# A decoder layer on one core: three value chunks and a gate chunk made as pairs by seven products, and three activation chunks split straight from PSUM

## The chip, the cores and the metric

The kernel runs on one core of a Trainium2 chip. The metric is device time in microseconds (us): the median of three runs of the kernel before was 1387.82 us (1387.64 to 1389.24). The profile shows one further execution of the same program. Its engines are named PE (matmul; PEld is its weight load), DVE (vector), ACT (scalar), POOL (GpSimd, here an issuer of DMAs) and SP (the issuer of the weight loads).

## What is computed

One layer of a decoder over 256 positions of width 2048, in float32. Cut to what matters:

```python
h = rmsnorm(x, g_mix)
proj = h @ w_in                                  # 2048 x 12288: q, k, v of 16 heads, then 3 gates of 2048
q, k, v = ...                                    # 16 heads of 128: groups 0 to 3 of four heads
gates = sigmoid(proj[..., 3 * MIX_WIDTH:])
o_a = stick_breaking_attention(q[:4], k[:4], v[:4])                     # group 0
o_b, o_c = moba_attention(...), dilated_attention(...)                  # groups 1 to 3, softmax with biases
merged = gates[0] * (o_a @ w_branch_a) + gates[1] * (o_b @ w_branch_b) + gates[2] * (o_c @ w_branch_c)
x = x + merged @ w_out
gu = rmsnorm(x, g_ffn) @ w_gu                    # 2048 x 11264
x = x + (silu(gu[..., :5632]) * gu[..., 5632:]) @ w_down
```

## The kernel before

Weights arrive from DRAM in blocks of 256 rows by 512 columns (a tile 128x1024, 512 KB). To keep float32 accuracy each block is split in two parts by `split` (lines 104 to 107): ACT writes a rounded copy `w_hi`, DVE the rest `w_lo`; the activations are kept as such parts too. `product` (line 164) then issues three matmuls of 512 columns, lines 167 to 169: high by high, high by low, low by high.

A chunk of 512 output columns is made in one of two ways.

- `project`, the plain way: 16 row tiles of the weights times 2 halves of the positions, 32 products, 96 matmuls, with 8 blocks split.
- `project_pair` makes two chunks at once. Over half of the rows (the chunks `WC` of the activations) it makes seven products of sums in place of eight of blocks, in the manner of Strassen and Winograd: `form` is one of the seven (12 matmuls), `rest` a plain block of the other half. That is 180 matmuls for two chunks, 22 splits, six additions of weight blocks on DVE (lines 321 and 310), two more by an accumulating DMA that POOL issues (line 360), four copies of PSUM banks by ACT (`snapshot`, line 305) and four additions of 128x512 that combine the results (lines 367, 369, 372, 380). `begin_pair` starts the loads and splits of the next pair ahead of time.

`units` sets the order of the projection: v of group 0, a gate chunk, q and k of groups 0 and 1 (a pair each, "qk"), v1, qk2, v2, qk3, v3, a gate chunk, and then the other gate chunks in pairs. Attention is woven in between: it is written as generators (`attention`, `rows_to_columns`) in the list `slow_stages`; `parts`, which splits a block, advances that list at every second call. Group g's attention is put in the list by `keep_v`, once v of the group is there. From the pair `chunks[4]` on, the list is drained and the attention's PSUM is given to `acc2`.

After the branches and the output projection come the eleven pairs over `w_gu` (loop over c, line 942). Each gives one chunk c of 512 columns of the activation a = silu(g) * u. `to_a` transposes it on PE into PSUM, copies it with ACT into SBUF (line 938) and sends it to the DRAM tensor `a_mem` by POOL's queue (line 939). `take_a` reads a chunk back (line 959, `a_raw<-a_mem`, 512 KB) and splits it into `a_hi` and `a_lo` for the down projection. It is called right behind the loop for the first three chunks (`EARLY`), whose tiles lie in the pool `pe`, and later for the rest. The instructions are not issued in the order in which they are written: a scheduler puts each engine's list in an order of its own when the program is built, and each engine then executes its list in that order. `tc.keep_in_program_order` pins some of them.

Of the kernel before, what the change touches and what calls it, by code (L numbers as in the profile page):

```python
# [9 lines left out]
F32 = mybir.dt.float32  # L10
# [7 lines left out]
P = 128  # L18
D = 2048
S = 256  # L20
NT = S // P
# [33 lines left out]
def hybrid_block(ctx: ExitStack, tc: tile.TileContext, x, g_mix, w_in, q_gain, k_gain, w_branch, w_out,  # L55
# [82 lines left out]
    def finish_stages(queue):  # L138
        while queue:
            advance(queue)  # L140
# [612 lines left out]
    def attention(g, qT, kT, v):  # L753
        biases = []
        if g:
            for hl in (0, 2):
                bias = pa.tile([P, 2, S], F32, name="bias")
                nc.gpsimd.dma_start(bias, bass.AP(tensor=vec.tensor, offset=vec.offset + (4 * g - H_A + hl) * NDIST,
                                                  ap=[[1, P], [NDIST, 2], [1, S]]))
                biases.append(bias)  # L760
        for hl in (0, 2):
            if g:
                yield from softmax_pair(4 * g + hl, hl, qT, kT, v, biases[hl // 2])
            else:
                yield from stick_breaking(hl, qT, kT, v)
            yield
# [9 lines left out]
    heads = {}  # L776

    def keep_v(g, ps):
        finish_stages(slow_stages)
        heads["v", g] = v = pa.tile([P, NT, NB], F32, name="v", bufs=1)  # L780
        for t in range(NT):
            nc.scalar.activation(v[:, t, :], ps[t], AF.Copy, scale=rstd[:, t:t + 1])
        if g:
            slow_stages.append(attention(g, *heads["qk", g], v))

    def keep_qk(g, q0, q1, k0, k1):
        sbs = []
        for t, (src, own) in enumerate(((q0, True), (q1, False), (k0, True), (k1, True))):
            sb = src if own else half_kb()
            nc.scalar.activation(sb, src, AF.Copy, scale=rstd[:, t % NT:t % NT + 1])  # L790
            sbs.append(sb)
        heads["qk", g] = qkT = [pa.tile([P, 4, S], F32, name=f"{n}T") for n in "qk"]
        if g:
            stages.append(rows_to_columns(g, sbs, qkT))
        else:
            slow_stages.append(rows_to_columns(g, sbs, qkT))
            slow_stages.append(attention(g, *qkT, heads["v", g]))

    chunks = [(c, b) for c in range(4) for b in range(3)]
    units = [("v", 0), ("gate", chunks[0]), ("qk", 0), ("qk", 1), ("v", 1), ("qk", 2), ("v", 2), ("qk", 3), ("v", 3)]
    units += [("gate", chunks[1])] + [("gates", chunks[i:i + 2]) for i in range(2, len(chunks), 2)]

    def gate_col(c, b):
        return 3 * NH * HD + b * D + c * NB

    def pair_of(kind, what):
        if kind == "qk":
            return hs, w_in, what * NB, NH * HD + what * NB  # L810
        if kind == "gates":
            return hs, w_in, gate_col(*what[0]), gate_col(*what[1])

    def in_turn():
        turn.reverse()
# [11 lines left out]
    others = in_turn  # L827
    ahead = None
    for (kind, what), after in zip(units, units[1:] + [(None, None)]):
        if kind == "gates" and what[0] == chunks[4]:  # L830
            finish_stages(slow_stages)
            pat.close()
            acc2 = ctx.enter_context(tc.tile_pool(name="acc2", bufs=1, space=PSUM))
            others = beside
            o = Columns(pool(ph1, "o", "left"), "o", NH)
            stages.append(split_o())
        nxt = pair_of(*after)
        if kind in ("qk", "gates"):
            ps, ahead = project_pair(*pair_of(kind, what), ahead, nxt)
            if others is in_turn:  # L840
                turn.reverse()
        else:
            ps = project(h, 0, w_in, 0, KT, V0 + what * NB if kind == "v" else gate_col(*what),
                         *((ps0, 4, there) if (kind, what) == ("v", 0) else ()))
            ahead = begin_pair(*nxt) if nxt else None
        finish_stages(stages)
        if kind == "v":
            keep_v(what, ps)
            if what == 0:
                slow_stages.append(sums_of_h())  # L850
        elif kind == "qk":
            keep_qk(what, *ps)
        elif kind == "gate":
            keep_gate(*what, ps)
        else:
            keep_gate(*what[0], ps[:2])
            keep_gate(*what[1], ps[2:])
# [73 lines left out]

    a_mem = dram.tile([NF // 4, P, 4, S], F32, name="a_mem")

    def to_a(c, srcs):
        for t in range(NT):
            pt = transpose4(srcs[t])
            st = half_kb().rearrange("p (k q) -> p k q", k=4)
            nc.scalar.copy(st, pt)
            nc.gpsimd.dma_start(a_mem[c, :, :, t * P:(t + 1) * P], st)
            yield  # L940
# [7 lines left out]
            nc.vector.scalar_tensor_tensor(sg[t], u, rstd2[:, t:t + 1], sg[t], op0=ALU.mult, op1=ALU.mult)  # L948
        stages.append(to_a(c, sg))

    WD = (4, 6, 8)
    ORDER = [0, 1, 2, 4, 3, 6, 5, 8, 7, 9, 10]
    EARLY = 3
    a = Chunks(None, "a", NF // 4, WD, False)

    def take_a(pl, c):
        a.place(pl, c)
        raw = pr.tile([P, 4, S], F32, name="a_raw", bufs=2)
# [6 lines left out]
        else:  # L965
            split(*a.t[c], raw)

    for c in ORDER[:EARLY]:
        take_a(pe, c)
    h2_stack.close()  # L970
    pd = pool(ctx, "pd", "left")

# [143 lines left out]
```

## Time and profile before

| What | Value |
|---|---|
| median of 3 runs | 1387.82 us |
| the profiled execution | 1387.56 us, its span 1385.8 us |
| PE busy | 1362.3 us (98%), 6404 matmuls |
| DVE busy | 1151.7 us (83%) |
| ACT busy | 880.9 us (64%) |
| POOL busy | 109.4 us (8%) |
| granted PE clock, mean | 0.994 |
| bytes moved by DMA | 331.07 MB |

The projections of `w_in` fill the span up to about 530 us, the branches and the output projection the time to about 700 us, the eleven pairs of `w_gu` the time to about 1160 us, and the down projection the rest. PE is near full everywhere, so what counts is where it is not: the rows on its waits and on the granted clock.

### The profile page before, as it was taken

To read this page: it belongs to the slowest core of one execution; us is meant where nothing else is said; L and a number is where in the kernel's file an instruction comes from. 1 tells how busy PE (TensorE), PEld (TensorE's weight loads), DVE (VectorE), ACT (ScalarE), POOL (GpSimd) and SP (SyncE) were. 2 spreads that over 40 slices of the span, in tenths; PEclk is the share of its full clock that TensorE was granted. 3 is DMA by queue.
4 is the path that set the end of the run, shared out by engine and by line. 5 is a ranking of instruction groups with operands and counts; after the bars stand their busy time and mean duration, and the time that the engine had idled before them with its cause. 6 is when DMAs were issued, how large, how long until landed. Compare 5 with 4: busy or idle time off the path is not lost.

```text
span 1385.8 us, 17910 instructions
## 1 busy us (share of the span) xinstructions
PE 1362.3 (98%) x6404; PEld 1184.9 (85%) x6404; DVE 1151.7 (83%) x1222; ACT 880.9 (64%) x1140; POOL 109.4 (8%) x173
## 2 busy tenths in 40 slices
PE   9999999999999999999999988999999999999998
PEld 7888888888888888888887877888888888788887
DVE  7888797858989987776698877999999998887785
ACT  7678877767776665445565656667666665564553
POOL 1100000000010112101001001010000010100000
PEclk9999999999999999999999999999999999999999
DMA  8875567576687779877887677678787877767553
GB/s 277 288 255 169 202 181 257 147 242 196 244 286 266 263 228 336 276 220 227 294 276 252 224 244 228 214 259 285 247 277 244 274 216 236 258 239 258 195 178 101
DMA packets 93928, 331.07 MB, mean 239 GB/s; under 512 B 11312, under 2 KB 12928, under 8 KB 93840
## 3 DMA queue, kind: packets, MB, share of 16 engines
q1 hardware_dynamic: 76896, 275.29, 57.1%
q0 software_dynamic: 15760, 53.60, 15.0%
q8 instruction: 50, 0.82, 0.2%
q10 hardware_dynamic: 1184, 1.06, 0.2%
q14 instruction: 38, 0.31, 0.1%
HBM read 292.65 MB, written 16.27 MB: 223 GB/s over the span
## 4 chain that ended last, share of the span: by engine, by line
PE 77%; issue 12%; DMA 4%; ACT 3%; DVE 3%; POOL 1%; POOLq 0%; ACTq 0%; DVEq 0%
PE ps L167 9%; PE ps L168 9%; PE ps L169 9%; PE qs L169 9%; PE qs L168 9%; PE qs L167 9%; PE z L167 4%; PE z L169 4%; PE z L168 4%; DMA a_raw<-a_mem 2%; PE v L167 2%; PE v L168 2%; PE v L169 2%; PE tr L189 1%; ACT w_hi L105 1%
## 5 line engine op out<-in xcount | busy, mean ns | idle before, releaser
L105 DVE TENSOR_TENSOR w_lo<-w_raw,w_hi 128x1024 fp32r<-128x1024 f32 x334 | 405.2, 1221 | 84.7 <-ACT w_hi L105 81.9
L105 ACT CAST w_hi<-w_raw 128x1024 fp32r<-128x1024 f32 x334 | 347.4, 1048 | 177.3 <-PE qs L169 80.1
L105 ACT CAST w_hi<-g_raw 128x1024 fp32r<-128x1024 f32 x184 | 191.5, 1048 | 137.0 <-DVE g_raw L310 45.8
L105 DVE TENSOR_TENSOR w_lo<-g_raw,w_hi 128x1024 fp32r<-128x1024 f32 x184 | 221.3, 1222 | 37.3 <-ACT w_hi L105 34.1
L105 ACT CAST w_hi<-u 128x1024 fp32r<-128x1024 f32 x138 | 143.8, 1047 | 82.9 <-PE qs L169 17.8
L105 DVE TENSOR_TENSOR w_lo<-u,w_hi 128x1024 fp32r<-128x1024 f32 x138 | 167.8, 1221 | 27.4 <-ACT w_hi L105 26.6
L168 PE MATMUL ps<-w_lo,h_hi 128*128 128x512 f32 x360 | 136.7, 380 | 0.0
L169 PE MATMUL ps<-w_hi,h_lo 128*128 128x512 f32 x360 | 136.4, 379 | 0.0
L167 PE MATMUL ps<-w_hi,h_hi 128*128 128x512 f32 x360 | 134.0, 383 | 0.0
L168 PE MATMUL qs<-w_lo,h_hi 128*128 128x512 f32 x332 | 126.4, 381 | 0.0
L169 PE MATMUL qs<-w_hi,h_lo 128*128 128x512 f32 x332 | 125.9, 380 | 0.0
L167 PE MATMUL qs<-w_hi,h_hi 128*128 128x512 f32 x332 | 122.5, 381 | 0.0
L169 PEld LDWEIGHTS ps<-w_hi,h_lo 128*128 128x128 f32 x360 | 68.0, 189 | 9.6
L168 PEld LDWEIGHTS ps<-w_lo,h_hi 128*128 128x128 f32 x360 | 68.1, 189 | 9.3
L167 PEld LDWEIGHTS ps<-w_hi,h_hi 128*128 128x128 f32 x360 | 67.8, 189 | 9.2
L321 DVE TENSOR_TENSOR u<-g_raw 128x1024 f32<-128x1024 f32 x40 | 48.8, 1219 | 26.7 <-DMA g_raw<-in_w_in 18.6
L169 PEld LDWEIGHTS qs<-w_hi,h_lo 128*128 128x128 f32 x332 | 62.8, 189 | 9.4 <-issue 0.6
L168 PEld LDWEIGHTS qs<-w_lo,h_hi 128*128 128x128 f32 x332 | 62.8, 189 | 9.0 <-DVE w_lo L105 0.4
L167 PEld LDWEIGHTS qs<-w_hi,h_hi 128*128 128x128 f32 x332 | 62.7, 189 | 8.6
L167 PE MATMUL v<-w_hi,h_hi 128*128 128x512 f32 x120 | 47.7, 397 | 13.3 <-ACT w_hi L105 13.3
L310 DVE TENSOR_TENSOR u<-u,g_raw 128x1024 f32<-128x1024 f32 x40 | 47.2, 1219 | 0.0
L310 DVE TENSOR_TENSOR g_raw<-g_raw 128x1024 f32<-128x1024 f32 x40 | 47.1, 1218 | 0.0
(398 smaller groups left out, 2950.2 us busy)
## 6 DMA issues: line engine op xcount, KB each, us to landing
w_raw<-in_w_in SPq DMA_DIRECT2D x118, 512.0 KB, 4.7
g_raw<-in_w_gu SPq DMA_DIRECT2D x88, 512.0 KB, 6.1
w_raw<-in_w_gu SPq DMA_DIRECT2D x88, 512.0 KB, 6.6
g_raw<-in_w_in SPq DMA_DIRECT2D x72, 512.0 KB, 6.2
w_raw<-in_w_down SPq DMA_DIRECT2D x64, 512.0 KB, 4.3
u<-g_raw POOLq DMA_DIRECT2D x40, 512.0 KB, 5.5
w_raw<-in_w_branch SPq DMA_DIRECT2D x32, 512.0 KB, 4.8
w_raw<-in_w_out SPq DMA_DIRECT2D x32, 512.0 KB, 4.3
```

Source lines behind the costliest of these rows:

```text
L105: for op in nc.scalar.copy(hi, src), nc.vector.tensor_sub(lo, src, hi.bitcast(F32)):
L167: nc.tensor.matmul(ps, ah, wh, start=start, stop=False, **how)
L168: nc.tensor.matmul(ps, ah, wl, start=False, stop=False, **how)
L169: nc.tensor.matmul(ps, al, wh, start=False, stop=stop, **how)
L189: nc.tensor.transpose(pt[:, i, :], src[:, i * P:(i + 1) * P], ident)
L310: tc.keep_in_program_order(nc.vector.tensor_add(d, d, a))
L321: nc.vector.tensor_add(d, a, b)
```

## The change

There are two parts.

1. v of groups 1 and 2 become one pair ("vv"), and v of group 3 with the gate chunk `chunks[1]` another ("vg"). v of group 2 is made ahead of qk2; until it is used it lies in the four heads of `o_raw` that group 3's output takes later. Attention of a group is put in the list by `attend`. The drain of `slow_stages` comes where v1, v2's attention and the pair `chunks[8]` need it; the attention's PSUM is handed over at `chunks[8]` in place of `chunks[4]`.
2. The first three chunks of a that the down projection takes are placed ahead of the loop, and `to_a` splits them from PSUM: no copy to SBUF, no trip to `a_mem` and back.

```diff
     def keep_v(g, ps):
-        finish_stages(slow_stages)
-        heads["v", g] = v = pa.tile([P, NT, NB], F32, name="v", bufs=1)
+        if g == 2:
+            v = o_raw[:, 12:16, :].rearrange("p h q -> p (h q)").rearrange("p (t n) -> p t n", t=NT)
+        else:
+            if g == 1:
+                finish_stages(slow_stages)
+            v = pa.tile([P, NT, NB], F32, name="v", bufs=1)
+        heads["v", g] = v
         for t in range(NT):
             nc.scalar.activation(v[:, t, :], ps[t], AF.Copy, scale=rstd[:, t:t + 1])
-        if g:
-            slow_stages.append(attention(g, *heads["qk", g], v))
+
+    def attend(g):
+        slow_stages.append(attention(g, *heads["qk", g], heads["v", g]))
...
-    units = [("v", 0), ("gate", chunks[0]), ("qk", 0), ("qk", 1), ("v", 1), ("qk", 2), ("v", 2), ("qk", 3), ("v", 3)]
-    units += [("gate", chunks[1])] + [("gates", chunks[i:i + 2]) for i in range(2, len(chunks), 2)]
+    units = [("v", 0), ("gate", chunks[0]), ("qk", 0), ("qk", 1), ("vv", (1, 2)), ("qk", 2), ("qk", 3)]
+    units += [("vg", (3, chunks[1]))] + [("gates", chunks[i:i + 2]) for i in range(2, len(chunks), 2)]
...
-        if kind == "gates" and what[0] == chunks[4]:
+        if kind == "gates" and what[0] == chunks[8]:
             finish_stages(slow_stages)
             pat.close()
...
-        if kind in ("qk", "gates"):
+        if kind in ("qk", "gates", "vv", "vg"):
             ps, ahead = project_pair(*pair_of(kind, what), ahead, nxt)
...
+        elif kind == "vv":
+            keep_v(1, ps[:2])
+            keep_v(2, ps[2:])
+            attend(1)
         elif kind == "qk":
+            if what == 3:
+                finish_stages(slow_stages)
+                attend(2)
             keep_qk(what, *ps)
+        elif kind == "vg":
+            keep_v(3, ps[:2])
+            keep_gate(*what[1], ps[2:])
+            attend(3)
...
+    for c in ORDER[:EARLY]:
+        a.place(pe, c)
+
     def to_a(c, srcs):
         for t in range(NT):
             pt = transpose4(srcs[t])
+            if c in ORDER[:EARLY]:
+                a.put(c, t, pt)
+                yield
+                continue
             st = half_kb().rearrange("p (k q) -> p k q", k=4)
             nc.scalar.copy(st, pt)
             nc.gpsimd.dma_start(a_mem[c, :, :, t * P:(t + 1) * P], st)
             yield
...
-    for c in ORDER[:EARLY]:
-        take_a(pe, c)
     h2_stack.close()
```

The order of the instructions moves at three places. The first is ACT's list in the second pair over `w_gu`. Names: `w_raw` and `g_raw` are weight blocks as loaded, `u` a sum of two, `w_hi` their rounded part, `tr` a PSUM bank with transposes, `sc` a scratch tile, `z` and `ps` PSUM banks; the number behind a name tells one tile from the next. Before:

```order
L938 COPY sc_6723<-tr_6718 128x512
L938 COPY sc_6741<-tr_6736 128x512
L105 CAST w_hi_6794<-u_6660 128x1024
L305 COPY sc_6750<-z_6686 128x512
L105 CAST w_hi_6804<-u_6661 128x1024
L105 CAST w_hi_6820<-w_raw_6818 128x1024
L105 CAST w_hi_6838<-g_raw_6648 128x1024
L105 CAST a_hi0_10162<-a_raw_10164 128x1024
L105 CAST w_hi_6848<-g_raw_6650 128x1024
L105 CAST w_hi_6862<-w_raw_6860 128x1024
```

With the change:

```order
L105 CAST a_hi0_6387<-tr_6797 128x4x128
L105 CAST a_hi0_6387<-tr_6814 128x4x128
L105 CAST w_hi_6871<-u_6739 128x1024
L305 COPY sc_6827<-z_6765 128x512
L105 CAST w_hi_6881<-u_6740 128x1024
L105 CAST w_hi_6897<-w_raw_6895 128x1024
L105 CAST w_hi_6915<-g_raw_6727 128x1024
L105 CAST w_hi_6925<-g_raw_6729 128x1024
L105 CAST w_hi_6939<-w_raw_6937 128x1024
```

The split of the reloaded chunk, which stood between two weight splits, is gone; the rounded part is taken from PSUM where the copy to scratch stood. The same holds for the third and fourth pair.

The second place is DVE's list at the end of the pair qk1, where the plain chunk v1 followed and now the pair vv begins (`p` with `att` is attention of group 0):

```order
 L372 TENSOR_TENSOR sc<-ps,sc 128x512
-L105 TENSOR_TENSOR w_lo<-w_raw,w_hi 128x1024 x4
+L105 TENSOR_TENSOR w_lo<-w_raw,w_hi 128x1024
+L321 TENSOR_TENSOR u<-g_raw 128x1024 x2
+L105 TENSOR_TENSOR w_lo<-w_raw,w_hi 128x1024
+L105 TENSOR_TENSOR w_lo<-g_raw,w_hi 128x1024 x2
 L664 TENSOR_TENSOR p<-p,att 128x768
```

Two additions of weight blocks for the next pair now stand here, among the splits.

The third is POOL's list over the pairs with attention: `bias` is a table for attention that one of two buffers takes, `u<-g_raw` the accumulating DMA of a pair.

```order
 L774 DMA gate_mem<-sc 128x512 x2
-L360 DMA u<-g_raw 128x1024 x4
+L360 DMA u<-g_raw 128x1024 x6
 L758 DMA bias<-vec 128x2x256
 L360 DMA u<-g_raw 128x1024 x2
-L758 DMA bias<-vec 128x2x256 x2
+L758 DMA bias<-vec 128x2x256
+L360 DMA u<-g_raw 128x1024 x2
+L758 DMA bias<-vec 128x2x256
 L360 DMA u<-g_raw 128x1024 x2
```

The pair vv puts two accumulating DMAs ahead of the third `bias`, and two more now stand between the fourth and the fifth.

More of the change, by code (lines that the diff above doesn't have):

```diff
@@ L796, in keep_qk @@
             slow_stages.append(rows_to_columns(g, sbs, qkT))
-            slow_stages.append(attention(g, *qkT, heads["v", g]))
+            attend(g)
     chunks = [(c, b) for c in range(4) for b in range(3)]
-    units = [("v", 0), ("gate", chunks[0]), ("qk", 0), ("qk", 1), ("v", 1), ("qk", 2), ("v", 2), ("qk", 3), ("v", 3)]
-    units += [("gate", chunks[1])] + [("gates", chunks[i:i + 2]) for i in range(2, len(chunks), 2)]
+    units = [("v", 0), ("gate", chunks[0]), ("qk", 0), ("qk", 1), ("vv", (1, 2)), ("qk", 2), ("qk", 3)]
+    units += [("vg", (3, chunks[1]))] + [("gates", chunks[i:i + 2]) for i in range(2, len(chunks), 2)]
     def gate_col(c, b):
@@ L812, in pair_of @@
             return hs, w_in, gate_col(*what[0]), gate_col(*what[1])
+        if kind == "vv":
+            return hs, w_in, V0 + what[0] * NB, V0 + what[1] * NB
+        if kind == "vg":
+            return hs, w_in, V0 + what[0] * NB, gate_col(*what[1])
     def in_turn():
@@ L932, in hybrid_block @@
     a_mem = dram.tile([NF // 4, P, 4, S], F32, name="a_mem")
+    WD = (4, 6, 8)
+    ORDER = [0, 1, 2, 4, 3, 6, 5, 8, 7, 9, 10]
+    EARLY = 3
+    a = Chunks(None, "a", NF // 4, WD, False)
+    for c in ORDER[:EARLY]:
+        a.place(pe, c)
     def to_a(c, srcs):
@@ L949, in hybrid_block @@
         stages.append(to_a(c, sg))
[L951 to L954, printed above, removed]
     def take_a(pl, c):
```

## The prediction

> **What bounds the kernel.** I read the page first, then PE's waits, then the timeline around the longest one, then the windows by stage.
>
> ```profile
> span 1385.8 us, 17910 instructions
> PE 1362.3 (98%) x6404; PEld 1184.9 (85%) x6404; DVE 1151.7 (83%) x1222; ACT 880.9 (64%) x1140; POOL 109.4 (8%) x173
> ```
>
> PE is the bound. Time can come from fewer matmuls, from its idle time (1385.8 less 1362.3, 23.5 us) or from a fuller clock. The list of PE's waits names one row that matters (total, times, longest):
>
> ```profile
> PE v L167 <- ACT w_hi L105: 13.3, 4, 4.2
> ```
>
> Three of the four are alike. Around the first, the timelines of ACT, POOL and PE (start, duration, what; in brackets the idle time ahead of it and who ended it):
>
> ```profile
> 754.40 1.04 ACT L105 CAST w_hi<-g_raw 128x1024 fp32r<-128x1024 f32 x1 [2.69 <-DVE g_raw L310]
> 759.96 1.04 ACT L105 CAST a_hi<-a_raw 128x1024 fp32r<-128x1024 f32 x1 [4.51 <-DMA a_raw<-a_mem]
> 760.91 1.04 ACT L105 CAST w_hi<-g_raw 128x1024 fp32r<-128x1024 f32 x1
> ...
> 747.60 1.62 POOL L939 DMA_DIRECT2D a_mem<-sc  x2 [32.20 <-ACT sc L938]
> 754.42 0.56 POOL L959 DMA_DIRECT2D a_raw<-a_mem  x1 [2.62 <-PE z L169]
> ...
> 758.40 0.38 PE L169 MATMUL z<-w_hi,h_lo 128*128 128x512 f32 x1
> 762.95 0.79 PE L167 MATMUL v<-w_hi,h_hi 128*128 128x512 f32 x1 [4.18 <-ACT w_hi L105]
> 763.54 0.63 PE L167 MATMUL z<-w_hi,h_hi 128*128 128x512 f32 x1
> 763.97 0.63 PE L167 MATMUL ps<-w_hi,h_shi 128*128 128x512 f32 x1
> ```
>
> A chunk of a is written to DRAM at 747.60 and read back at 754.42. ACT stands before the split of the reloaded chunk, with the weight splits queued behind it, until 759.96; PE has used up what was split and waits 4.18 us. Then its matmuls start 0.43 us apart instead of 0.22. The windows by pair, from transpose to transpose (length, then busy time and count of PE, PEld, DVE, ACT and POOL, then PE's granted clock, DMA share, GB/s), show the price: three disturbed pairs, one undisturbed, all with 189 matmuls, and the slow piece behind the first wait.
>
> ```profile
> 746.08:792.86 46.78, 42.60 (x189) 36.59 (x188) 38.13 (x36) 27.51 (x31) 3.83 (x5) 0.93 0.69 225
> 792.86:838.49 45.63, 41.39 (x189) 35.75 (x188) 37.78 (x36) 27.51 (x31) 3.83 (x5) 0.96 0.70 231
> 838.49:885.16 46.67, 42.47 (x189) 36.51 (x188) 37.91 (x36) 27.50 (x31) 3.84 (x5) 0.93 0.68 226
> 885.16:924.89 39.73, 39.73 (x189) 34.82 (x188) 36.61 (x35) 26.68 (x30) 3.29 (x4) 1.00 0.76 252
> ...
> 762.95:768.23 5.28, 5.28 (x12) 4.20 (x13) 4.24 (x5) 3.37 (x4) 0.00 (x0) 0.50 0.51 161
> ```
>
> **Part 1, the activation chunks.** The three disturbed pairs take 46.78 + 45.63 + 46.67 = 139.08 us, against 3 x 39.73 = 119.19. If nothing else holds them, 19.89 us come back: about 12.6 of idle PE (three waits of 4.2) and 7.3 of half clock. ACT's list, shown above, no longer has the split that waited: the chunk's new splits stand where the copies to scratch stood, released by the same transposes. What they cost, by these groups (mean ns behind the busy time):
>
> ```profile
> L938 ACT COPY sc<-tr 128x512 f32<-128x512 f32 x22 | 12.9, 589 | 14.0 <-PE tr L189 13.4
> L105 ACT CAST m_hi<-tr 128x512 fp32r<-128x512 f32 x8 | 4.3, 593 | 0.1
> L105 DVE TENSOR_TENSOR m_lo<-tr,m_hi 128x512 fp32r<-128x512 f32 x8 | 5.1, 682 | 0.0
> L105 DVE TENSOR_TENSOR a_lo<-a_raw,a_hi 128x1024 fp32r<-128x1024 f32 x8 | 9.8, 1223 | 18.1 <-ACT a_hi L105 18.1
> ```
>
> The output projection's input is already split from PSUM in this form, at 593 ns on ACT and 682 ns on DVE. Six ACT copies (589) become six ACT splits (593), and three ACT splits of a reloaded block go: ACT gains. DVE has 2 x 0.68 = 1.36 us in each pair where 1.22 stood. Beside the undisturbed 36.61 that is 37.97 of 39.73 us, 95.6% busy. One pair in the trace is as dense:
>
> ```profile
> 706.40:746.08 39.68, 39.06 (x179) 33.06 (x177) 38.57 (x47) 27.59 (x31) 1.78 (x2) 1.00 0.85 293
> ```
>
> 38.57 us of DVE in 39.68, with 0.62 us of PE idle. So the new splits cost from nothing to 0.62 in each pair; I take 0.5 in all. The DMAs that go (six writes and three reads on POOL's queue) have nothing but the accumulating DMA behind them; they are worth nothing more. The transposes' PSUM bank is held 0.68 us longer; the next transposes are a pair away.
>
> The clock belongs to the saving, so a rule is weighed here. The row has 5.28 us at 0.50 behind the first wait. The Trainium skill (TensorE: Matmul & The Clock Gate, Part 1) says that PE falls to half clock after an idle window of some 3.4 us and regains it after about as long at work. The trace agrees on the halving. By that figure a stall would cost, as an estimate, 4.2 us and half of 3.4, the three 17.7 us in place of 19.9, and the forecast would be 2.2 us higher.
>
> **Part 2, the pairs.** Two plain chunks are 192 matmuls, a pair 180; two pairs save 24. A pair of gate chunks without attention gives the price, 38.85 us for 180 matmuls, 0.2158 each:
>
> ```profile
> 449.20:488.05 38.85, 38.85 (x181) 34.02 (x180) 34.90 (x33) 26.50 (x31) 4.02 (x6) 1.00 0.81 270
> ```
>
> So 24 x 0.2158 = 5.18 us go from PE. SP loads the same 16 blocks for two chunks either way.
>
> The other engines get more. Each new pair adds on DVE six splits, six block additions and four additions of 128x512; on ACT six splits and four bank copies; on POOL two DMA issues.
>
> ```profile
> L105 DVE TENSOR_TENSOR w_lo<-u,w_hi 128x1024 fp32r<-128x1024 f32 x138 | 167.8, 1221 | 27.4 <-ACT w_hi L105 26.6
> L367 DVE TENSOR_TENSOR sc<-sc 128x512 f32<-128x512 f32 x20 | 13.7, 685 | 0.9 <-ACT sc L305 0.9
> L105 ACT CAST w_hi<-u 128x1024 fp32r<-128x1024 f32 x138 | 143.8, 1047 | 82.9 <-PE qs L169 17.8 <-PE ps L169 15.1 <-DVE u L1016 14.0
> L305 ACT COPY sc<-qs 128x512 f32<-128x512 f32 x35 | 20.3, 581 | 3.0 <-PE qs L169 2.8
> 925.57 2.35 DVE L310 TENSOR_TENSOR u<-u,g_raw 128x1024 f32<-128x1024 f32 x2
> ```
>
> Two block operations in a row take 2.35 us, so the second adds 1.13. DVE gets 12 x 1.13 to 1.22 and 4 x 0.685 per pair, 16.3 to 17.4; I take 33.8 us for both. ACT gets 6 x 1.05 + 4 x 0.58 = 8.6, 17.2 for both. The place is the stretch from the end of qk0 to the end of the first gate pair; the second row reaches to the end of the gates, the third is the densest undisturbed stretch of the later stages.
>
> ```profile
> 93.67:371.25 277.58, 276.01 (x1355) 241.53 (x1354) 221.88 (x277) 209.49 (x364) 11.05 (x14) 1.00 0.63 205
> 93.67:526.90 433.23, 430.94 (x2070) 376.43 (x2069) 360.88 (x404) 316.50 (x485) 28.13 (x40) 1.00 0.69 224
> 1000.00:1050.00 50.00, 50.00 (x241) 43.84 (x241) 46.70 (x45) 34.91 (x41) 5.75 (x7) 1.00 0.72 238
> ```
>
> Afterwards the stretch has 277.6 - 5.2 = 272.4 us for PE and 221.9 + 33.8 = 255.7 us for DVE: 93.9%, where 46.70 of 50 us, 93.4%, ran with no PE idle. ACT has 226.7, 83%. DVE is thus just within what it has carried, and some attention can move into the later gate pairs, since the list is now drained at `chunks[8]`. A good part of DVE's idle time before was the plain chunks' own:
>
> ```profile
> 146.39 1.23 DVE L321 TENSOR_TENSOR u<-g_raw 128x1024 f32<-128x1024 f32 x1 [5.92 <-DMA g_raw<-in_w_in]
> 356.22 1.23 DVE L321 TENSOR_TENSOR u<-g_raw 128x1024 f32<-128x1024 f32 x1 [0.62 <-DMA g_raw<-in_w_in]
> ```
>
> At 146 us, in the plain v1, DVE waits 5.92 us for the next pair's blocks; where a pair follows a pair, 0.62. The new waits cost, below, -2.3 us (the PE idle of the long stretch, 433.23 less 430.94, vanishes); above, if DVE could again be used only 221.88/277.58 = 80%, 255.7/0.80 = 319.9 us, 42.3 more than before. The nearest row is the dense one without PE idle, so I take 1.0.
>
> POOL's two more issues per pair hide in an engine that is 8% busy. They stand behind `bias` loads that wait for attention:
>
> ```profile
> 177.00 0.74 POOL L758 DMA_DIRECT2D bias<-vec  x1 [70.22 <-DVE p L689]
> 178.13 0.86 POOL L360 DMA_DIRECT2D u<-g_raw  x1 [0.39 <-DVE w_lo L105]
> ```
>
> The `bias` load waited 70.22 us, and the accumulating DMA behind it went 0.39 us after that by a later DVE instruction. In the new list one `bias` stands before each pair's two again, and in DVE's list the read that frees it precedes the split that frees `u`: no cost. Without that cover `u` comes late and PE waits, at the price of a stall (below).
>
> **The sum**, on the profiled execution of 1387.56 us (0.26 below the median of the runs): 1387.56 - 19.89 + 0.5 - 5.18 + 1.0 = 1363.99. I say 1364.
>
> **Rivals.**
> A. One or two real stalls in the dense stretch. A disturbed pair costs (139.08 - 119.19)/3 = 6.63 us, idle and half clock. For it: DVE near full, attention's tied chain of ACT and DVE, scratch and PSUM shared with a pair at work. Against: two operations of blocked ACT or DVE are covered by five buffers of split weights. Without waits the time is 1362.5; one stall gives 1369.1, two 1375.8.
> B. The wait in the three pairs takes another form, such as DVE late by its denser list. For it: 95.6% busy. Against: 706.40. Half of 19.89 lost gives 1364 + 9.9 = 1373.9.
> C. Half clock behind the waits comes for another reason, and only the 12.6 us of idle return: 1371.3. Against: full clock in the pair without a wait.
> D. The other side: DVE stays at 80% in the stretch, because its idle time is latency and not PE's pace. Then 1387.56 - 19.89 + 42.3 = 1410, slower. It decides from 19.9 us of loss on, where DVE gets no further than 255.7/297.5 = 86%. Against it are the 93.4% above.
> E. It doesn't do what it says: pairs, but some reloaded split still ahead of weight splits: 1382. The list of ACT speaks against it.
>
> **How the numbers follow.** The forecast with waits of -2.3 to +4 us (1360.2 to 1366.5) 0.60; A 0.25 (one stall 0.17, more 0.08); B 0.06; C 0.02; D 0.04; E 0.02; something better than the forecast's floor 0.01. The range from 1359.5 to 1372 takes in the forecast, one stall and C and leaves some 0.2 out. 0.2% is 2.8 us, about what a measurement of this kernel can tell: faster is all but D and a sliver of E's and B's tails, 0.95; same 0.01; slower 0.04.
>
> **What would show it.** Right: the three windows at 39.7 to 40.4 us with clock 1.00; the wait of PE on `w_hi` down from 13.3 to under 2 us; 6380 matmuls; the stretch from qk0 to the last gates at 427 to 431 us with DVE some 34 us busier. Wrong: a new row among PE's waits above 3 us with a clock below 1.00 between 94 and 380 us (A or D), PE waiting on `w_lo` in the pairs of `w_gu` (B).

## The result, and the profile after

The changed kernel takes 1379.41 us (median of 4 runs, 1376.54 to 1380.63), the kernel before 1387.73 us (4 runs on the same chip, 1386.44 to 1389.24). The ratio is 0.9937, 95% interval 0.9918 to 0.9955. It is faster by 8.3 us, where the sum gave 23.6, and the time lies above the range of 1359.5 to 1372. The direction was right, the size was not.

The page of the changed kernel, span and engines:

```profile
span 1377.2 us, 17903 instructions
PE 1353.8 (98%) x6380; PEld 1176.5 (85%) x6380; DVE 1180.5 (86%) x1257; ACT 891.3 (65%) x1155; POOL 106.2 (8%) x168
```

The count of matmuls is the forecast one. The windows of the first three pairs over `w_gu`, from transpose to transpose (columns as in the prediction):

```profile
758.40:798.12 39.72, 39.72 (x189) 34.82 (x188) 37.55 (x37) 26.47 (x30) 1.71 (x2) 1.00 0.74 239
798.12:837.85 39.73, 39.73 (x189) 34.83 (x188) 37.24 (x37) 26.56 (x30) 1.71 (x2) 1.00 0.72 238
837.85:877.58 39.73, 39.73 (x189) 34.82 (x188) 37.49 (x37) 26.56 (x30) 1.71 (x2) 1.00 0.74 239
```

No idle PE, clock 1.00, 119.18 us in place of 139.08: the first part did what it should. The loss is in the other place. The stretch from the end of qk0 to the end of the gates, then five of its pairs (vv, qk3, vg, and the gate pairs `chunks[4]` and `chunks[8]`):

```profile
93.52:540.42 446.90, 430.53 (x2045) 372.31 (x2044) 391.57 (x435) 329.85 (x502) 31.52 (x44) 1.00 0.68 222
...
139.17:188.94 49.77, 45.34 (x220) 38.46 (x219) 43.73 (x56) 38.66 (x75) 1.70 (x2) 1.00 0.58 189
...
232.38:280.48 48.10, 44.43 (x213) 37.70 (x212) 40.00 (x48) 36.59 (x72) 1.71 (x2) 1.00 0.59 196
280.48:332.22 51.74, 48.27 (x231) 41.58 (x230) 45.53 (x65) 39.74 (x87) 3.21 (x4) 0.97 0.62 193
...
376.66:420.69 44.03, 41.83 (x196) 35.73 (x195) 39.26 (x36) 32.92 (x38) 3.98 (x6) 1.00 0.71 240
...
464.44:501.57 37.13, 34.53 (x158) 29.51 (x157) 32.85 (x31) 24.82 (x28) 4.01 (x6) 1.00 0.78 260
```

Before, this stretch took 433.23 us with 2.29 us of idle PE. Now it takes 446.90 with 16.37 idle, although it has two dozen matmuls fewer. DVE is not full in any of these pairs (43.73 of 49.77 us in vv). PE's waits there, by line and engine waited for (total, times, longest):

```profile
PE ps L167 <- ACT w_hi L105: 3.4, 3, 2.0
PE tr L189 <- DVE qT L748: 2.8, 2, 1.4
PE ps L168 <- DVE w_lo L105: 1.9, 3, 0.9
PE qs L168 <- DVE w_lo L105: 1.6, 2, 1.3
PE z L168 <- DVE w_lo L105: 1.6, 1, 1.6
PE qs L167 <- ACT w_hi L105: 1.6, 1, 1.6
PE tr L189 <- DVE sc L739: 1.1, 2, 0.6
PE qs L167 <- ACT sc L305: 0.9, 1, 0.9
PE v L168 <- DVE w_lo L105: 0.8, 1, 0.8
PE tr L189 <- ACT pT L711: 0.6, 1, 0.6
PE v L167 <- ACT w_hi L105: 0.2, 1, 0.2
```

They are 18 waits, the longest of 2.0 us: no stall like those that went, but many small ones, part of them for split weights, part for the transposes of q and k. By place, 11.57 us of the idle time lie in vv, qk3 and vg; the other 4.80 lie in the two gate pairs, beside which nothing of the normalising runs any more (its last copy starts at 308.7 us).

What stands ahead of such a wait is seen in vv. It now runs beside the normalising of group 1's q and k (`rows_to_columns`), which is a chain over three engines: 16 squares with sums on ACT (L730), the root (DVE L174, ACT L176 and L177, eight small DVE operations), four scalings on DVE (L739), transposes on PE, copies back. The timelines of ACT, DVE and PE:

```profile
141.93 0.31 ACT L730 ACTIVATE sc<-sc 128x128 f32<-128x128 f32 x1
...
143.89 0.19 ACT L730 ACTIVATION_READ_ACCUMULATOR sc<-sc 128x1 f32 x1
...
144.75 1.99 ACT L105 CAST w_hi<-w_raw 128x1024 fp32r<-128x1024 f32 x2
...
156.25 1.28 ACT L177 ACT_TABLE_LOAD   x1
...
161.67 1.04 ACT L105 CAST w_hi<-g_raw 128x1024 fp32r<-128x1024 f32 x1 [1.49 <-DVE g_raw L310]
...
145.82 2.36 DVE L105 TENSOR_TENSOR w_lo<-w_raw,w_hi 128x1024 fp32r<-128x1024 f32 x2 [3.02 <-ACT w_hi L105]
...
160.42 1.22 DVE L310 TENSOR_TENSOR g_raw<-g_raw 128x1024 f32<-128x1024 f32 x1
...
162.77 0.16 DVE L183 TENSOR_TENSOR rr<-rs_y,rs_t 128x16 f32<-128x16 f32 x1
...
163.99 2.48 DVE L739 TENSOR_TENSOR sc<-sc,rr 128x512 f32<-128x512 f32 x4
...
162.77 0.48 PE L167 MATMUL ps<-w_hi,b_shi 128*128 128x512 f32 x1 [2.00 <-ACT w_hi L105]
164.12 0.48 PE L168 MATMUL ps<-w_lo,b_shi 128*128 128x512 f32 x1 [0.87 <-DVE w_lo L105]
```

Seven squares stand in a row on ACT, from 141.93 on, then a copy and one more; the weight split behind them starts at 144.75, and DVE sits idle for 3.02 us until it has that. Later DVE works on attention and the root, the block sum at 160.42 comes behind them, ACT waits 1.49 us for that sum, and PE 2.00 for ACT. So the engines wait for one another in turn, while each is idle now and then. The experiments ask which of it is the cause.

### The profile page after: what moved, and what is told of

It reads as the page before. It is cut to its first block, busy times and chain, and to the rows that moved or that the text cites. A ratio compares the mean times of both kernels' runs of the same rounds, so it can differ in the third digit from the quotient of the medians.

```text
span 1377.2 us, 17903 instructions
## 1 busy us (share of the span) xinstructions
PE 1353.8 (98%) x6380; PEld 1176.5 (85%) x6380; DVE 1180.5 (86%) x1257; ACT 891.3 (65%) x1155; POOL 106.2 (8%) x168
## 5 line engine op out<-in xcount | busy, mean ns | idle before, releaser
L105 DVE TENSOR_TENSOR w_lo<-w_raw,w_hi 128x1024 fp32r<-128x1024 f32 x318 | 385.7, 1220 | 75.8 <-ACT w_hi L105 73.8
L105 ACT CAST w_hi<-w_raw 128x1024 fp32r<-128x1024 f32 x318 | 331.2, 1049 | 155.2 <-PE qs L169 69.4
L105 ACT CAST w_hi<-g_raw 128x1024 fp32r<-128x1024 f32 x200 | 208.5, 1049 | 151.1 <-PE ps L169 43.6
L105 DVE TENSOR_TENSOR w_lo<-g_raw,w_hi 128x1024 fp32r<-128x1024 f32 x200 | 239.1, 1221 | 36.2 <-ACT w_hi L105 33.7
L105 ACT CAST w_hi<-u 128x1024 fp32r<-128x1024 f32 x150 | 156.3, 1046 | 91.9 <-PE ps L169 22.1
L105 DVE TENSOR_TENSOR w_lo<-u,w_hi 128x1024 fp32r<-128x1024 f32 x150 | 181.5, 1220 | 34.1 <-ACT w_hi L105 33.4
L168 PE MATMUL ps<-w_lo,h_hi 128*128 128x512 f32 x336 | 128.4, 382 | 0.0
L169 PE MATMUL ps<-w_hi,h_lo 128*128 128x512 f32 x336 | 127.5, 380 | 0.1
L167 PE MATMUL ps<-w_hi,h_hi 128*128 128x512 f32 x336 | 124.3, 383 | 0.9 <-ACT w_hi L105 0.9
L360 POOL DMA_DIRECT2D u<-g_raw x44 | 38.6, 877 | 315.6 <-DVE w_lo L105 228.4
```

The costliest lines, as they stand in the source:

```text
L105: for op in nc.scalar.copy(hi, src), nc.vector.tensor_sub(lo, src, hi.bitcast(F32)):
L167: nc.tensor.matmul(ps, ah, wh, start=start, stop=False, **how)
L168: nc.tensor.matmul(ps, ah, wl, start=False, stop=False, **how)
L169: nc.tensor.matmul(ps, al, wh, start=False, stop=stop, **how)
L360: nc.gpsimd.dma_start(d, a, accum_op=ALU.add)
```

## The experiments

All ran on the chip with the kernel before beside them; its median was 1387.7 to 1389.2 us in every group, so that a difference of a microsecond between groups says nothing. The rivals in the expectations: A, the load on DVE summed over the stretch; L, a loss local to a pair; S, the squares on ACT that stand ahead of weight splits.

**Each part alone.** e1_chunks_only has `units`, `keep_v` and the handover as before and the changed `to_a`; e2_pairs_only is its counterpart.

```diff
-    units = [("v", 0), ("gate", chunks[0]), ("qk", 0), ("qk", 1), ("vv", (1, 2)), ("qk", 2), ("qk", 3)]
+    units = [("v", 0), ("gate", chunks[0]), ("qk", 0), ("qk", 1), ("v", 1), ("qk", 2), ("v", 2), ("qk", 3), ("v", 3)]
-    units += [("vg", (3, chunks[1]))] + [...]
+    units += [("gate", chunks[1])] + [...]
```

> Part 1 of the change alone: the first three activation chunks are split from PSUM, the projections stay as before (v1, v2, v3 and the gate chunk plain). If the two parts add up and part 1 is worth what the windows of the three pairs say, 19.9 us come back: 1387.7 - 19.9 + 0.5 = 1368.3, faster than the changed kernel by 11. Rival: part 1 brings only the 8.3 us that the whole change measured and the pairs are neutral: 1379.4.

> Part 2 alone: the pairs vv and vg, with the three chunks still sent to DRAM and read back. If the parts add up, the changed kernel's 1379.4 and the 19.9 us of the reload stalls: 1399.3, slower than before by 11.6, with some 16 us of idle PE between 94 and 540 us. Rival: the pairs are neutral and the reload stalls shrink for another reason: 1387.7.

e1_chunks_only: 1366.57 us (1365.15 to 1367.26), ratio 0.9842 (0.9827 to 0.9856). e2_pairs_only: 1403.2 us, ratio 1.011 (1.0093 to 1.0127), slower. The first part gives some 22 us and the second takes some 13 to 15 away. e1_chunks_only does all the work and is the fastest such kernel of this study; it beats both kernels. Its span, and its stretch:

```profile
span 1364.4 us, 17884 instructions
...
93.57:526.79 433.22, 430.72 (x2069) 376.42 (x2068) 360.75 (x403) 316.31 (x484) 28.07 (x40) 1.00 0.69 224
```

The stretch is that of before to 0.01 us.

**One new pair alone.** Both keep the first part. e3_vv_only leaves v3 and the gate chunk plain, e4_vg_only leaves v1 and v2 plain; the calls of `attend` and, in e4_vg_only, `keep_v` go with them.

```diff
# e3_vv_only
-    units += [("vg", (3, chunks[1]))] + [...]
+    units += [("v", 3), ("gate", chunks[1])] + [...]
# e4_vg_only
-    units = [..., ("qk", 1), ("vv", (1, 2)), ("qk", 2), ("qk", 3)]
+    units = [..., ("qk", 1), ("v", 1), ("qk", 2), ("v", 2), ("qk", 3)]
```

> The changed kernel with only the pair vv: v3 and the gate chunk are plain again and stand behind qk3. Theory L (local): PE stalls where the normalising of q and k, which follows each qk pair, falls on a pair and not on a plain chunk, so the stalls in vv (4.4 us idle) and in qk3 (3.7) stay and the one behind qk3 (3.5 idle, half clock of some 1.7) goes; 12 matmuls more are 2.6: about 1379.4 + 2.6 - 6 = 1376. Theory A (average): DVE is too full over the whole stretch, so with 17 us of DVE work less nearly all of its stalls go: about 1368.3 - 2.6 + 1.5 = 1367.

> The changed kernel with only the pair vg: v1 stands plain behind qk1 and v2 behind qk2, as before. Theory L: the stalls in vv and qk3 go, the one behind qk3 stays (5 to 6 us with refill and clock), and what is lost in the later gate pairs (4.8 idle) may stay: 1368.3 - 2.6 + 6 = 1372, up to 1377. Theory A: 17 us of DVE work less, nearly all stalls go: about 1367.

1377.51 us, ratio 0.9919 (0.9905 to 0.9934), and 1376.82 us, ratio 0.9922 (0.9899 to 0.9944): each pair alone costs 10 to 11 us against e1_chunks_only, both together 12.8. The costs are not additive. Part of them is half clock behind a wait: summed as (1 - clock) times length over windows of 2 us in the stretch, 5.1 us in e3_vv_only, 1.7 in e4_vg_only and 1.7 in the changed kernel. With a sum of DVE's load (A) one pair would have cost about nothing; L comes near (it gave 1376, and 1372 to 1377). e4_vg_only up to 280 us, where its order is still that of the kernel before, and behind that:

```profile
93.50:280.00 186.50, 184.93 (x907) 161.23 (x906) 153.66 (x193) 142.56 (x246) 8.19 (x10) 1.00 0.63 204
280.00:540.00 260.00, 251.42 (x1171) 216.73 (x1170) 224.71 (x229) 185.34 (x253) 22.72 (x34) 0.99 0.72 235
```

8.58 us of idle PE behind, 1.57 ahead, as in the kernel before.

**The steps of the normalising.** e5_no_squares sets the sums of squares to a constant; e6_no_norm_dve keeps the squares and leaves out the root and the scalings.

```diff
# e5_no_squares
+            nc.vector.memset(ss, float(HD))
             for i, sb in enumerate(sbs):
-                junk = half_kb()
-                for hd in range(4):
-                    cols = slice(hd * HD, (hd + 1) * HD)
-                    nc.scalar.activation(junk[:, cols], sb[:, cols], AF.Square, accum_out=...)
                 yield
# e6_no_norm_dve
-            rr = pa.tile([P, 4 * NT * 2], F32, name="rr", bufs=1)
-            rsqrt_mean(rr, ss, HD, 4 * NT * 2)
...
-                nc.vector.tensor_mul(sb3, sb3, rr[:, 4 * i:4 * i + 4, None].to_broadcast([P, 4, HD]))
```

> The changed kernel without the squares of q and k on ACT (16 for each of groups 1 to 3, some 5 us of ACT each); the sums get a constant, so the normalising has the wrong scale; DVE's work stays. Theory S: the squares, which come in a row between the weight splits of the pair behind each qk pair, starve DVE of split input (3 us idle in vv at 143 us), DVE is then late for the middle of the pair, and PE waits. Then most of the 11.6 us of idle PE in vv, qk3 and vg go, with their refill and half clock: 1379.4 - 13 = 1366 to 1369. Theory A (DVE too full on average) gives no change: 1379.

> The changed kernel with the squares, but without what follows them: the chain of small DVE and ACT steps for the root (with its table loads) and the four scalings of 128x512 on DVE, some 4 us of DVE and 3 of ACT for each of groups 1 to 3; q and k are left unscaled. Theory A: with 12 us of DVE less the average falls from 88% to 84% and most of the stalls go, 1368. Theory S: the starving by the squares stays, the late DVE has less to catch up with; about half of the idle time goes: 1373.

1362.11 us, ratio 0.981 (0.9795 to 0.9825), and 1364.2 us, ratio 0.9826 (0.9809 to 0.9844). The windows of the stretch in the two:

```profile
94.20:522.60 428.40, 427.11 (x2046) 370.97 (x2045) 387.21 (x410) 312.49 (x398) 31.54 (x44) 1.00 0.71 231
```

```profile
94.40:525.50 431.10, 427.75 (x2045) 372.48 (x2044) 380.41 (x397) 323.26 (x493) 31.54 (x44) 1.00 0.70 230
```

Without the squares, DVE does 387.21 us in 428.40, 90.4%, with 1.29 us of idle PE: the pairs' own load fits, as the prediction had it, and A falls. But S, too, is only half of it: with all the squares in place and nothing that uses them, 1364.2 is as good as free, where S gave 1373. Either end of the chain can be taken away, and the loss goes. The second of the two runs also takes work off DVE (380.41 us in place of 391.57), so that the runs further down, which keep the work, have to tell chain from load.

**Spreading and moving.** e7_slow_norm puts `rows_to_columns` into the list that is advanced half as often, and attention of group 2 behind qk3. e8_vv_early makes vv ahead of qk1 and puts single plain chunks behind qk1 and qk2.

```diff
# e7_slow_norm
-            stages.append(rows_to_columns(g, sbs, qkT))
+            slow_stages.append(rows_to_columns(g, sbs, qkT))
# e8_vv_early
-    units = [..., ("qk", 0), ("qk", 1), ("vv", (1, 2)), ("qk", 2), ("qk", 3)]
+    units = [..., ("qk", 0), ("vv", (1, 2)), ("qk", 1), ("gate", chunks[1]), ("qk", 2), ("v", 3), ("qk", 3)]
```

> The changed kernel, all of its work, with the normalising and transposing of q and k (groups 1 to 3) in the slow list, which is advanced at every second weight split and not at every one, so that the same steps are spread over about a whole pair. Theory S: the splits come between shorter rows of squares, the idle PE in vv, qk3 and vg falls to about half: 1372. Theory A: no change, 1379; if attention is late by it, up to 1384.

> All of the work, with another order: v0, gate, qk0, the pair vv, qk1, gate (plain), qk2, v3 (plain), qk3, gate pairs. Group 0 has no normalising, so no squares fall on vv; behind qk1 and qk2 stands a plain chunk; only those of group 3 fall on a pair. One pair saves 2.6 us against part 1 alone (1366.6). Theory S: one stall of some 5 us and what the late handover of the attention's PSUM costs (3): 1366.6 - 2.6 + 8 = 1372. Theory A: one pair less than the change and thus little idle: 1365. If any added pair in this stretch costs what the single pairs cost (10 to 11): 1377.

1373.19 us, ratio 0.9892 (0.9876 to 0.9909), and 1379.93 us, ratio 0.994 (0.9925 to 0.9955). Spacing the same work gives 6 us back; moving one pair away from the normalising gives none, although e8_vv_early has only this one new pair. vv itself then has no idle PE. It lies elsewhere: 3.35 us between 140 and 185 us (in qk1, ahead of the first square at 190.7 us), 3.89 between 318 and 360 (behind qk3) and 5.6 from 400 us on, in gate pairs. So a pair can stall without the normalising beside it; this run also starts the attention of groups 1 to 3 at other places, and the two effects are not told apart.

**The squares on another engine, or in fewer instructions.** Three kernels with all work kept.

```diff
# e9_pool_squares (e10_pool_norm also has the scalings on gpsimd)
-                    nc.scalar.activation(junk[:, cols], sb[:, cols], AF.Square, accum_out=...)
+                nc.gpsimd.tensor_mul(junk, sb, sb)
+                j3 = junk.rearrange("p (h d) -> p h d", h=4)
+                w = HD // 2
+                while w > 1:
+                    nc.gpsimd.tensor_add(j3[:, :, :w], j3[:, :, :w], j3[:, :, w:2 * w])
+                    w //= 2
+                nc.gpsimd.tensor_add(ss[:, 4 * i:4 * i + 4, None], j3[:, :, 0:1], j3[:, :, 1:2])
# e11_one_square
-                    nc.scalar.activation(junk[:, cols], sb[:, cols], AF.Square, accum_out=...)
+                nc.scalar.activation(junk, sb, AF.Square)
+                nc.vector.tensor_reduce(ss[:, 4 * i:4 * i + 4], junk.rearrange("p (h d) -> p h d", h=4), ...)
```

> All work is kept; the squares of q and k of groups 1 to 3 and their sums (16 ACT instructions in a row per group) are made by POOL, one product of 128x512 and seven additions of halves per tile. If what delays PE is the room that these squares take in ACT's list between the weight splits, the time comes to that of the kernel without squares, 1362 to 1365. If it is the lateness of the whole chain from q and k to the transposes, or the total work, POOL's longer chain helps nothing: 1375 to 1382. POOL also issues the accumulating DMAs of the pairs, and these now stand behind its arithmetic: if that decides, the time is above 1380.

> As the kernel with the squares on POOL, and POOL also multiplies q and k by the reciprocal roots (four instructions of 128x512 per group, on DVE before). If both ACT's and DVE's part of the normalising count, this is the best of the versions that keep all work, 1361 to 1364, at or below the version that changes the activation chunks alone (1366.6). If the squares were all of it, it equals the version with only the squares on POOL. If POOL's queue becomes the wait, a new row of PE or DVE waiting for POOL appears and the time is above 1370.

> All work is kept; the four squares with sums per tile become one square of 128x512 on ACT and one reduction on DVE: some 6.2 us of ACT per group become 2.3, and DVE gets four reductions of about 0.6 each. If the number of ACT instructions in a row is what counts, 1364 to 1368. If the load of both engines together is what counts, DVE's added 2.4 us per group eat part of it: 1368 to 1374. If neither, 1377 to 1380.

1405.65 us, ratio 1.0129 (1.0113 to 1.0145); 1406.14 us, ratio 1.0134 (1.0118 to 1.015); 1379.59 us, ratio 0.9947 (0.9928 to 0.9965). ACT is rid of the squares in e9_pool_squares, and the time rises by 26 us. PE's waits in its stretch, two rows, and the DVE row behind them:

```profile
PE tr L189 <- DVE sc L742: 19.7, 2, 10.9
PE ps L167 <- ACT w_hi L105: 8.2, 1, 8.2
...
DVE rs_v L174 <- POOL ss L734: 18.4, 3, 9.1
```

The lists keep the places of the root, the scalings and the transposes; POOL's sums come later, and now DVE stands 9.1 us before the root and PE 10.9 before a transpose, with everything behind them. So a link of the chain that comes late holds the whole list of its engine. Not all of the 26 us is that, though: the granted clock of the whole execution is 0.984 where the changed kernel has 0.999, and DVE, busy for 1192.2 us in place of 1180.5, is slowed beside POOL (last section). With the scalings on POOL too (e10_pool_norm) it is no better. In e11_one_square the busy time on its page is 885.2 us on ACT and 1187.1 on DVE, 6.1 less and 6.6 more than in the changed kernel, not the 3.9 less per group that I had expected of ACT; nothing is won. Its window of 150 to 200 us shows DVE full, with the added reductions:

```profile
150.00:200.00 50.00, 46.91 (x224) 39.44 (x223) 49.75 (x64) 34.77 (x44) 3.29 (x4) 1.00 0.61 200
```

**Chain or load.** e12_cut_chain keeps the instructions, but feeds the root a constant; the scheduler then puts the small root chains at the start of the lists. e13_spaced_steps keeps the chain and all work and lets three more steps pass ahead of the root and three behind it.

```diff
# e12_cut_chain
+            nc.vector.memset(ss, float(HD))
-                                         accum_out=ss[:, 4 * i + hd:4 * i + hd + 1])
+                                         accum_out=sq[:, 4 * i + hd:4 * i + hd + 1])
# e13_spaced_steps
+            for _ in range(3):
+                yield
             rr = pa.tile([P, 4 * NT * 2], F32, name="rr", bufs=1)
             rsqrt_mean(rr, ss, HD, 4 * NT * 2)
-            yield
+            for _ in range(4):
+                yield
```

> All instructions are kept, but the root takes a constant in place of the sums of squares (the scale of q and k is thereby wrong), so that nothing waits for the squares; the small root chain goes to the start of the lists, and the squares, the scalings, the transposes and their copies stay. If what delays PE is the chain of steps that wait for one another across ACT, DVE and PE in lists of fixed order, the time is that without squares, 1362 to 1365. If it is the room that the squares take on ACT, 1375 to 1380.

> All work is kept; three more steps of the list lie between the squares and the root and three between the root and the scalings, so that each link of the chain is asked for about 6 us later. If the chain of waiting steps is the cause and the lists follow this spacing, 1363 to 1372. If load is the cause, or the scheduler puts the links where it did, 1377 to 1382.

1369.38 us, ratio 0.9866 (0.9849 to 0.9882), and 1371.28 us, ratio 0.9879 (0.9865 to 0.9894). Their stretches:

```profile
94.00:528.70 434.70, 427.39 (x2045) 371.20 (x2045) 387.81 (x411) 323.55 (x493) 31.58 (x44) 1.00 0.69 228
```

```profile
93.50:531.30 437.80, 428.38 (x2045) 370.53 (x2044) 389.65 (x436) 331.25 (x505) 31.57 (x44) 1.00 0.69 226
```

e12_cut_chain lies between its two expectations: without the links 10 us come back, and 7 remain to the 1362.1 of e5_no_squares. In e13_spaced_steps nothing is taken away, ACT and DVE do as much as in the changed kernel (331.25 and 389.65 us, 329.85 and 391.57 there), and idle PE falls from 16.37 to 9.42 us. Where it falls shows more than the total:

| Kernel | idle PE up to 376 us, beside the normalising | from there to the end of the gates |
|---|---|---|
| e1_chunks_only | 1.78 | 0.72 |
| changed kernel | 11.57 | 4.80 |
| e6_no_norm_dve | 0.37 | 2.98 |
| e12_cut_chain | 2.52 | 4.79 |
| e13_spaced_steps | 4.14 | 5.28 |
| e7_slow_norm | 4.71 | 5.41 |
| e5_no_squares | 0.64 | 0.65 |

Beside the normalising, cutting the links or spacing them takes most of the idle time away. What stays in e12_cut_chain and e13_spaced_steps lies for the larger part in the gate pairs, where no square runs, so it is not the squares' room on ACT there.

**Both at once.** e14_spread_squares has two steps between the squares of one tile and the next and one more ahead of the root and behind it. e15_vg_spaced is e4_vg_only with the spacing of e13_spaced_steps.

```diff
# e14_spread_squares
-                yield
+                for _ in range(2):
+                    yield
+            yield
             rr = pa.tile([P, 4 * NT * 2], F32, name="rr", bufs=1)
             rsqrt_mean(rr, ss, HD, 4 * NT * 2)
-            yield
+            for _ in range(2):
+                yield
```

> All work is kept; two steps of the list instead of one between the squares of one tile and the next, and one more ahead of the root and behind it. In ACT's list the squares then stand in groups of four or eight with a weight split between them. If the loss is of two halves, the squares' room on ACT (about 7 us) and the chain (about 10 us), both are relieved here and the time falls below that of the spaced chain (1371): 1364 to 1369. If spacing helps the chain alone, 1370 to 1374. If load alone counts, 1377 to 1382.

> All work is kept; only v of group 3 and the gate chunk are a pair, v of groups 1 and 2 are plain as before, and the root and the scalings are asked for three steps later each. Without spacing this one pair made 1376.8, 10 us more than with no new pair (1366.6). If the chain's spacing decides there too, 1366 to 1370, and a value below 1366.6 would beat the change of the activation chunks alone; if not, 1375 to 1378.

1372.34 us, ratio 0.9887 (0.9868 to 0.9905), and 1373.15 us, ratio 0.9893 (0.9878 to 0.9909). Neither reaches its better case. Spreading the squares does no more than the other spacing (idle PE 4.17 us up to 376 us and 5.92 behind), and the single pair vg gets 3.7 of its 10 us back.

## Why the prediction was wrong, step by step

| Step | Forecast | Measured |
|---|---|---|
| part 1: three pairs over `w_gu` | -19.89 | -19.90 (119.18 in place of 139.08) |
| part 1: new splits | +0.5 | no idle PE in these pairs |
| part 1, elsewhere | 0 | about -1.2; -1.0 more behind the three pairs, of which e1_chunks_only has 0.2 |
| part 2: matmuls | 24 fewer, -5.18 | 24 fewer |
| part 2: new waits | +1.0 | +18.85 |
| profiled execution | 1363.99 | 1379.11 |

**Part 1 was right**, the clock included. The wait on the reloaded chunk was the cause of idle time and half clock, since both went with it. The estimate of 17.7 us for the three stalls, which the prediction set beside its 19.9, was too low. Some 2.2 us more came outside of the three pairs: from the last gates to the first transposes 217.98 us where 219.18 stood, and behind the three pairs 499.62 where 500.64 stood. e1_chunks_only has the first of these too (217.97; 0.62 us of idle PE are gone there), but hardly the second (500.45). The prediction had counted neither, and their cause is open.

**The step that failed is the term for new waits in part 2**, 1.0 us. The stretch was forecast at 433.23 - 5.18 + 1.0 = 429.05 and took 446.90: 17.85 us more, the term being 18.85. Of the 17.85, 13.08 are idle PE (16.37 in place of 2.29 + 1.0) and 4.77 are matmuls that took longer: 430.53 us busy, where 430.94 - 5.18 = 425.76 were due. Some 1.7 us of the 4.77 are half clock: 4.01 us at 0.57 in vg (last section), where the kernel before has full clock in the whole stretch. The other 3 are about what more waits cost: a matmul behind a wait shows 0.48 us, where one in the stream costs 0.2158, and 14 waits more than before (18 in place of 4) by 0.26 are, as an estimate, 3.6.

The estimate rested on the wrong likeness. I compared DVE's share of the stretch, 93.9%, with a dense stretch of 93.4% that ran without idle PE. That stretch has weight splits, sums of blocks and of results and the product with u, and no normalising. The average was not the trouble: with the same pairs, e5_no_squares runs at 90.4% of DVE with 1.29 us of idle PE, and the changed kernel at 391.57/446.90 = 87.6% with 16.37. What I did not cost was the chain of the normalising: in the kernel before, most of it fell on the plain v1, v2 and v3, in which DVE has about half the work (16 splits for two chunks, in place of 22 splits, six sums of blocks and four of results). ACT's list of the kernel before, in v1, has all 16 squares of group 1 in a row ahead of a weight split:

```profile
140.12 0.31 ACT L730 ACTIVATE sc<-sc 128x128 f32<-128x128 f32 x1
...
144.80 1.98 ACT L105 CAST w_hi<-w_raw 128x1024 fp32r<-128x1024 f32 x2
```

PE does not wait for it. The very idle time of DVE that I read there (5.92 us before the sum at 146 us) and booked as waste spans these squares: it was the slack that let the chain run without holding PE. In vv, eight squares in the same place leave DVE idle for 3.02 us with a denser list behind it, and later in the pair PE waits. So this is shown: beside the normalising the idle time needs the links that wait for one another (11.57 us; 0.37 in e6_no_norm_dve, 2.52 in e12_cut_chain), and it shrinks when the same work is spaced (4.14 in e13_spaced_steps, 4.71 in e7_slow_norm). e9_pool_squares points the same way, with two other causes in it. For the 4.80 us in the gate pairs this is not shown.

**The rivals.** A had the place right for the larger part, but the form wrong: not one or two stalls of 6.63 us, but 18 waits of 0.9 us on average. D had the mechanism, DVE's idle time as latency and not PE's pace, and too high a price: the stretch was to grow by 42.3 us by an average and grew by 13.67 (446.90 less 433.23), where from 19.9 on it would have made the kernel slower. I gave it 0.04, since I tested it with another average. B, C and E did not come about. That POOL's queue costs nothing held as far as the rows show: none of PE's, ACT's or DVE's waits in the stretch names the accumulating DMA.

The sign that the prediction named for a wrong forecast, a row of PE's waits above 3 us with a clock below 1.00 between 94 and 380 us, came only in part: no single wait reaches 3 us, but the row of `ps` on `w_hi` sums to 3.4 in three waits (2.5 of them in this span), and the clock of vg is 0.97. The sum over all rows would have been the clear sign.

**What is open.** The totals, 10 us for the links and 7 beyond them, hold for taking them away in that order; e6_no_norm_dve, in which the squares stay, would put only 2 on the squares, and e14_spread_squares, which was to relieve both, gained no more than e13_spaced_steps. So the share of the squares' room is not shown. e12_cut_chain also moves the root's table loads (1.28 us each) out of the stretch, so that these are counted with the links.

The idle time in the gate pairs is open too. Its first two waits (0.88 and 1.33 us, at 397 to 400 us) come behind the split of `o_raw`, four copies on ACT (3.89 us from 391.02 on) and four rests on DVE (4.62 us) that stand among the weight splits; the others (2.60 us together) are in the pair `chunks[8]`, for `z` and `v`, the banks that are handed over there. But e5_no_squares has this split and this handover too and shows 0.65 us, and the kernel before has the split at 366 us and no wait of PE from 360 to 376 us. Neither was tried by itself. As e5_no_squares reaches 1362.11, where the prediction gave 1362.5 without waits, the handover at `chunks[8]` need not cost anything.

In e15_vg_spaced, 6.6 us of one pair's cost are not explained by the spacing that was tried; attention's own chain beside the pair is the next suspect, and e8_vv_early, which stalls in qk1 beside attention alone, speaks for it.

## What to carry to other kernels

Before plain work is replaced by denser work, look at which chain of dependent steps runs beside it: the idle time of an engine there may be what hides the chain's latency, and its average load says nothing about that. Test the estimate against a stretch that carries the same chain, not against the densest one. Where such a chain must stay, ask for its links later, with other work between them, before taking work off it: the same instructions, spaced, gave 8 of 17 us back, while moving part of it from ACT to DVE gave none and moving it to POOL cost 26, half clock and a slowed DVE included.

## What the runs showed of the hardware

**Broken idle time and the clock.** Two places of the changed kernel have nearly the same idle time, in two pieces with one matmul between. Windows over each, and behind each:

```profile
160.77:164.12 3.35, 0.49 (x2) 0.19 (x1) 3.35 (x6) 2.28 (x3) 0.00 (x0) 1.00 1.03 259
164.12:169.99 5.87, 5.19 (x27) 4.38 (x28) 5.87 (x8) 4.54 (x6) 0.00 (x0) 1.00 0.06 13
302.54:305.96 3.42, 0.49 (x2) 0.19 (x1) 3.42 (x6) 2.87 (x3) 0.00 (x0) 1.00 0.42 123
305.96:309.97 4.01, 4.01 (x15) 3.49 (x16) 4.01 (x5) 3.13 (x5) 0.00 (x0) 0.57 0.00 0
```

2.86 us idle in 3.35 left the clock at 1.00, 2.93 in 3.42 were followed by 4 us at 0.57. No single wait there was longer than 2.0 us. The Trainium skill (TensorE: Matmul & The Clock Gate, Part 1) says that the clock goes by the activity in a free-running window of about 3.4 us, which does not start anew with a kernel. One place hit and the other not would fit that, but two places don't show it, and they differ: ahead of the second, PE had already waited 0.53 us and done only eight transposes since.

**POOL's arithmetic slows DVE.** In e9_pool_squares, while POOL adds, two DVE operations in a row, each of two inputs, take 3.61 us and the next two 3.15 us, where two take 2.35 us in the kernel before:

```profile
143.25 3.61 DVE L105 TENSOR_TENSOR w_lo<-w_raw,w_hi 128x1024 fp32r<-128x1024 f32 x2
146.78 3.15 DVE L310 TENSOR_TENSOR u<-u,g_raw 128x1024 f32<-128x1024 f32 x2
...
144.07 8.82 POOL L732 TENSOR_TENSOR sc<-sc 128x256 f32<-128x256 f32 x12
```

The Trainium skill (SBUF — State Buffer, Who interferes with whom) says that a DVE instruction with two inputs in SBUF contends with a GpSimd instruction that reads SBUF, through a read interface that the two share. The trace agrees in that DVE gets slower beside POOL, here by a factor of 1.3 to 1.5.
